# The vector engine in source order through the mixer of an encoder, with the convolution's taps between the pieces of weights

## The chip, the cores and the metric

The kernel runs on one core of a Trainium2 chip. A core has five engines that matter here, each with a queue of instructions of its own: TensorE (PE, matrix products and transposes), VectorE (DVE), ScalarE (ACT), GpSimd (POOL) and SyncE (SP, which issues most transfers). An engine works its queue strictly in order and waits on semaphores for what the others produce. The metric is the device time of one execution in microseconds, the median over several. Less is better.

## The reference

What is computed is a two-layer encoder over 256 tokens of width 1024, all in float32. One layer is a half step of a SwiGLU feed-forward block, the mixer, a second half step of feed-forward, and a gated embedding. The change lies in the mixer alone:

```python
u = rms_norm(h, norm_mix[i])
q, k, v, c, g = jnp.split(u @ w_in[i], splits, axis=-1)     # 512, 128, 128, 1024, 2048

q = rms_norm(q.reshape(B, S, N_HEADS, HEAD_DIM), q_norm[i])   # 8 heads of 64
k = rms_norm(k.reshape(B, S, KV_HEADS, HEAD_DIM), k_norm[i])  # 2 heads of 64
y_attn = window_attention(q, k, v, sink[i], rel_bias) @ w_attn_out[i]

c_val, c_gate = jnp.split(c, 2, axis=-1)
c = c_val * jax.nn.sigmoid(c_gate)
c = depthwise_conv(c, conv_w[i], conv_b[i])                   # 31 taps, 512 channels
c = jax.nn.silu(layer_norm(c, conv_ln_g[i], conv_ln_b[i]))
y_conv = c @ w_conv_out[i]

g_attn, g_conv = jnp.split(jax.nn.sigmoid(g), 2, axis=-1)
h = h + (g_attn * y_attn + g_conv * y_conv) @ w_o[i]
```

So attention and the convolution both come out of the same projection, run independently of each other, and meet in the last line.

## The kernel before

All products are float32 by three passes. Each weight is split into a high part, which ACT casts (`w_hi`, L104), and a low part, which DVE subtracts (`w_lo`, L105); PE then adds up high times high, low times high and high times low (L310 to L312). The class `Weights` streams the weights through this. A unit is one load of up to 1 MB into one of 5 raw buffers, issued by SP; a piece is half a unit or so, split into one of 8 pairs of `w_hi` and `w_lo`. Each `get()` prepares pieces up to 7 ahead of the one it hands out, and first runs the functions that were left with `later(n, fn)`, n calls earlier. The weights of attn_out and conv_out are used as they lie in their raw buffers, so such a buffer stays taken until PE has done with it.

The mixer, `mix`, runs in this order of source: two pieces of the convolution's input (`conv_in`, `ps_c`), queries (`ps_q`), keys and values (`ps_kv`), four chunks of gates (`ps_g`) into which the four blocks of attention are woven by `later` (scores `ps_s`, probabilities transposed `ps_pt`, products with the values `ps_o`), then attn_out (`ps_ao`), the layer norm of the convolution (transposes `ps_yt`, norm `yn`, transposes back `ps_yc`, a silu), conv_out (`ps_co`), and the merged product with w_o (`ps_up`), whose end prepares the second feed-forward block.

DVE has four kinds of work here. It subtracts the low parts. It runs the convolution: 30 taps for each of 4 groups of 128 channels (tap 0 goes to ACT), each a multiply-add over 256 tokens into `y`, 120 instructions a layer (L581). It normalizes the heads: a reduction, an addition, ten dependent small steps of an inverse square root (Newton's steps, `rh` and `nwt`), and four products, for q (`qn`) and for k (`kn`). And it runs the running maximum of the scores (L727) and the layer norm by token.

A scheduler orders the instructions of all engines at build time. It takes each instruction by a priority, which by default follows the source, and by a simulated time at which its operands are there. Before, two settings bend this in the mixer: the taps are given a priority 800 later than where they stand (`BACKGROUND`), and the preparation of weights one 100 later (`WEIGHTS_LAG`). The head norms and the layer norm run in `with_urgency`, which raises their priority.

Of the kernel before, what the change touches and what calls it, by code (L numbers as in the profile page):

```python
# [27 lines left out]
KC = CD // P  # L28
TAPS = 31
# [6 lines left out]
N = 512  # L36
LOOK = 7
RAW_BUFS = 5
BACKGROUND = 800
WEIGHTS_LAG = 100  # L40
ATTN = 5
W_BUFS = 8
DOWN_TAIL = 3
# [2 lines left out]
class Weights:  # L46
# [3 lines left out]
    def __init__(self, tc, raw_pool, w_pool):  # L50
        self.tc, self.nc = tc, tc.nc
        self.raw_pool, self.w_pool = raw_pool, w_pool
        self.units, self.specs = [], []
        self.raw, self.ready, self.held, self.hooks = {}, {}, {}, []
        self.next_load = self.next_prep = self.next_get = 0
        self.rest, self.pin, self.lag = 0, None, 0

    def unit(self, k, n, sources):
        self.units.append((k, n, sources))
# [24 lines left out]
    def prep_upto(self, i):  # L84
        nc = self.nc
        while self.next_prep <= min(i, len(self.specs) - 1):
            k, n, pieces, as_is = self.specs[self.next_prep]
            for u, *_ in pieces:
                self.load_upto(u + RAW_BUFS - 2)
                if u >= self.next_load:  # L90
                    return
            if as_is:
                ((u, k0, s0, _, w),) = pieces
                self.ready[self.next_prep] = (self.raw[u][:, k0 : k0 + k, s0 : s0 + w],)
                self.next_prep += 1
                continue
            hi = self.w_pool.tile([P, 2 * N], F32R, name="w_hi")
            lo = self.w_pool.tile([P, 2 * N], F32R, name="w_lo")
            hv = hi[:, : k * n].rearrange("p (k n) -> p k n", n=n)
            lv = lo[:, : k * n].rearrange("p (k n) -> p k n", n=n)  # L100
            for u, k0, s0, d0, w in pieces:
                src = self.raw[u][:, k0 : k0 + k, s0 : s0 + w]
                parts = (
                    nc.scalar.copy(out=hv[:, :, d0 : d0 + w], in_=src),  # L104
                    nc.vector.tensor_tensor(  # L105
                        out=lv[:, :, d0 : d0 + w],
                        in0=src,
                        in1=hv[:, :, d0 : d0 + w].bitcast(F32),
                        op=ALU.subtract,
                    ),  # L110
                )
                if self.pin:
                    for ins in parts:
                        self.pin(ins)
                    self.pin = None
            self.ready[self.next_prep] = (hv, lv)
            self.next_prep += 1

# [9 lines left out]
    def get(self):  # L128
        i = self.next_get
        due = [fn for at, fn in self.hooks if at <= i]  # L130
        self.hooks = [h for h in self.hooks if h[0] > i]
        for fn in due:
            fn()
        p0 = self.tc.cur_priority
        self.tc.cur_priority = p0 + self.lag
        self.prep_upto(i + LOOK - self.rest)
        self.tc.cur_priority = p0
        self.next_get += 1
        return self.ready.pop(i)


@with_exitstack
def encoder_kernel(ctx: ExitStack, tc: tile.TileContext, a: dict, out: bass.AP):
# [12 lines left out]
    def acc_tile(name):  # L156

        return accp.tile([P, NT, N], F32, name=name, tag="acc")
# [4 lines left out]
    def tok(t):  # L163
        return slice(t * P, (t + 1) * P)
# [45 lines left out]
    ws = Weights(tc, raw_pool, w_pool)  # L210
# [351 lines left out]
    def mix(l, st, nxt):  # L562
        u = st.x
        cw, kg, bias, sink = (late[n] for n in ("cw", "kg", "bias", "sink"))
        with tc.tile_pool(name="mix_pool", bufs=1) as mp:
            cpad = mp.tile([P, KC, T + 2 * PAD], F32, name="cpad", tag="cpad")
            nc.gpsimd.memset(cpad[:, :, 0:PAD], 0.0)
            nc.gpsimd.memset(cpad[:, :, PAD + T :], 0.0)
            y = mp.tile([P, KC, T], F32, name="y")
            background = tc.cur_priority + BACKGROUND  # L570
            ws.lag = WEIGHTS_LAG

            def tap(i, t):
                src = cpad[:, i, t : t + T]
# [11 lines left out]
            def conv_in(i):  # L586

                acc = acc_tile("ps_c")

                def evac():  # L590
                    cc = tmp.tile([P, NT, 256], F32, name="hh")
                    for t in range(NT):
                        sg = tmp.tile([P, 256], F32, name="sg")
                        nc.scalar.activation(out=sg, in_=acc[:, t, 256:], func=AF.Sigmoid, scale=st.rt(t))
                        nc.vector.scalar_tensor_tensor(
                            out=cc[:, t, :], in0=acc[:, t, :256], scalar=st.rt(t), in1=sg, op0=ALU.mult, op1=ALU.mult
                        )

                    def turn_c():
                        ps = tr_tile("ps_ct").rearrange("p (f t) -> p f t", f=2)  # L600
                        for f in range(2):
                            for t in range(NT):
                                nc.tensor.transpose(ps[:, f, tok(t)], cc[:, t, f * P : (f + 1) * P], ident)
                        nc.scalar.copy(out=cpad[:, i : i + 2, PAD : PAD + T], in_=ps)
                        p0 = tc.cur_priority
                        for t in range(TAPS):
                            for f in range(2):
                                tc.cur_priority = background + KC * t + i + f
                                tap(i + f, t)
                        tc.cur_priority = p0  # L610

                    ws.later(1, turn_c)

                chunk(acc, KD, u)
                pending.append(evac)
# [172 lines left out]
            def squash(c):  # L788
                for t in range(NT):
                    gs = g[:, t, c * N : (c + 2) * N]  # L790
                    tc.keep_in_program_order(nc.scalar.activation(out=gs, in_=gs, func=AF.Sigmoid))

            for c in range(4):
                gates(c)

# [12 lines left out]
            yn = mp.tile([P, NT, N], F32, name="yn", tag="pTs", bufs=2)  # L808

            def ln_by_token():  # L810
                for t in range(NT):
                    ps = tr_tile("ps_yt")
                    for i in range(KC):
                        nc.tensor.transpose(ps[:, i * P : (i + 1) * P], y[:, i, tok(t)], ident)
                    six = tmp.tile([P, 6], F32, name="six")
                    nc.vector.bn_stats(out=six, in_=ps)
                    mv = tmp.tile([P, 2], F32, name="mv")
                    nc.vector.bn_aggr(out=mv, in_=six)
                    rs = tmp.tile([P, 1], F32, name="rs")
                    nc.vector.tensor_scalar(  # L820
                        out=mv[:, 1:2], in0=mv[:, 1:2], scalar1=1e-5, scalar2=None, op0=ALU.add
                    )
                    rsqrt(rs, mv[:, 1:2], 1)
                    nc.vector.tensor_scalar(
                        out=yn[:, t, :], in0=ps, scalar1=mv[:, 0:1], scalar2=rs, op0=ALU.subtract, op1=ALU.mult
                    )
                table(AF.Silu)
# [59 lines left out]
                xs = x_tok[:, t, cols(c)]  # L887
                nc.vector.tensor_tensor(out=xs, in0=acc[:, t, :], in1=xs, op=ALU.add)

            ws.lag = 0  # L890
            return update(nxt(), KD, (Halves(ym[0]), Halves(ym[1])), add, 2)


# [119 lines left out]
```

## Time and profile before

| what | value |
|---|---|
| median of 3 runs | 1212.34 us (1212.13 to 1212.96) |
| the profiled execution's own time | 1212.65 us |
| its span | 1210.9 us |
| PE busy | 1155.3 us, 95% |
| DVE busy | 736.9 us, 61% |
| ACT busy | 583.2 us, 48% |
| TensorE's mean granted clock | 0.977 of full speed |
| mixer of layer 0, from the first `ps_c` to the second feed-forward's first product | about 214 to 391 us |

A row of a timeline gives the start in the span, the duration, engine, line, operation, the tile written and the tiles read, the shape, how many alike stand in a row, and in brackets how long the engine idled before and what ended that. Where an engine's rows stand close together, their durations overlap by a little, so a queue of them is shorter than the sum.

### The profile page before, as it was taken

How to read it: one execution, taken by the hardware profiler on the slowest of the kernel's cores; microseconds unless marked ns; L12 is line 12 of the kernel's file. 1: busy time of each engine (PE TensorE's matmuls, PEld its weight loads, DVE VectorE, ACT ScalarE, POOL GpSimd, SP SyncE). 2: the span in 40 equal slices, each digit the busy share in tenths (PEclk: the TensorE clock that was granted, in tenths of full speed). 3: DMA queues.
4: the chain of work that ended last, by engine and by line, in shares of the span. 5: the costliest groups of instructions: out<-in, count | busy, mean ns of one | idle time of the engine just before them, and what ended most of it. 6: DMA issues, size and time to landing. Idle time of an engine off the chain costs nothing.

```text
span 1210.9 us, 13444 instructions
## 1 busy us (share of the span) xinstructions
PE 1155.3 (95%) x5074; PEld 906.0 (75%) x5074; DVE 736.9 (61%) x1187; ACT 583.2 (48%) x803; POOL 5.7 (0%) x21
## 2 busy tenths in 40 slices
PE   8999999949999999999999999999399999999998
PEld 6878888836647888888878888888276588888786
DVE  7555554799546655555675555557994375555544
ACT  7444444525734544444555544446177255445432
POOL 0000000000000000000000000000000000000000
PEclk9999999978999999999999999999699999999999
DMA  9866555551354565555646555565323546555520
GB/s 318 275 207 213 180 170 186 182 137 35 105 164 157 180 189 188 158 190 173 209 150 198 182 183 191 176 195 162 94 70 104 173 151 200 180 183 178 178 87 35
DMA packets 155356, 202.47 MB, mean 167 GB/s; under 512 B 5283, under 2 KB 108787, under 8 KB 155292
## 3 DMA queue, kind: packets, MB, share of 16 engines
q1 hardware_dynamic: 154204, 200.57, 52.4%
q10 hardware_dynamic: 1088, 1.05, 0.3%
q8 instruction: 40, 0.66, 0.2%
q14 instruction: 24, 0.20, 0.1%
HBM read 200.53 MB, written 1.06 MB: 166 GB/s over the span
## 4 chain that ended last, share of the span: by engine, by line
PE 90%; DVE 7%; issue 1%; ACT 1%; DMA 1%; ACTq 0%; DVEq 0%
PE ps_gu L310 13%; PE ps_gu L312 13%; PE ps_gu L311 13%; PE ps_up L310 8%; PE ps_up L311 8%; PE ps_up L312 8%; DVE y L581 4%; PE ps_co L306 2%; PE ps_g L310 2%; PE ps_ao L306 2%; PE ps_g L311 2%; PE ps_g L312 2%; PE ps_h L521 2%; PE ps_s L718 2%; PE ps_x L358 1%; PE ps_pe L312 1%
## 5 line engine op out<-in xcount | busy, mean ns | idle before, releaser
L105 DVE TENSOR_TENSOR w_lo<-raw,w_hi 128x1024 fp32r<-128x1024 f32 x360 | 439.6, 1224 | 356.9 <-ACT w_hi L104 356.3
L104 ACT CAST w_hi<-raw 128x1024 fp32r<-128x1024 f32 x360 | 376.6, 1051 | 412.9 <-PE ps_gu L312 202.9
L311 PE MATMUL ps_up<-w_lo,hh 128*128 128x512 f32 x352 | 139.4, 396 | 0.0
L312 PE MATMUL ps_up<-w_hi,hl 128*128 128x512 f32 x352 | 139.4, 396 | 0.0
L310 PE MATMUL ps_up<-w_hi,hh 128*128 128x512 f32 x352 | 139.3, 396 | 0.0
L581 DVE SCALAR_TENSOR_TENSOR y<-cpad,cw,y 128x256 f32<-128x256 f32 x240 | 101.7, 478 | 0.0
L312 PEld LDWEIGHTS ps_up<-w_hi,hl 128*128 128x128 f32 x352 | 66.0, 188 | 16.1
L310 PEld LDWEIGHTS ps_up<-w_hi,hh 128*128 128x128 f32 x352 | 66.0, 188 | 15.8
L311 PEld LDWEIGHTS ps_up<-w_lo,hh 128*128 128x128 f32 x352 | 66.0, 188 | 15.7
L311 PE MATMUL ps_gu<-w_lo,x0h 128*128 128x512 f32 x176 | 70.6, 401 | 0.0
L312 PE MATMUL ps_gu<-w_hi,x0l 128*128 128x512 f32 x176 | 70.2, 399 | 0.0
L312 PE MATMUL ps_gu<-w_hi,xn0l 128*128 128x512 f32 x176 | 69.1, 395 | 1.2 <-DVE xn0l L348 1.2
L310 PE MATMUL ps_gu<-w_hi,x0h 128*128 128x512 f32 x176 | 69.9, 397 | 0.0
L311 PE MATMUL ps_gu<-w_lo,xn0h 128*128 128x512 f32 x176 | 69.6, 395 | 0.0
L311 PE MATMUL ps_gu<-w_lo,xf0h 128*128 128x512 f32 x176 | 69.5, 395 | 0.0
L311 PE MATMUL ps_gu<-w_lo,xf1h 128*128 128x512 f32 x176 | 69.5, 395 | 0.0
L310 PE MATMUL ps_gu<-w_hi,xn0h 128*128 128x512 f32 x176 | 69.2, 393 | 0.0
L310 PE MATMUL ps_gu<-w_hi,xf1h 128*128 128x512 f32 x176 | 69.1, 393 | 0.0
L310 PE MATMUL ps_gu<-w_hi,xf0h 128*128 128x512 f32 x176 | 69.1, 393 | 0.0
L312 PE MATMUL ps_gu<-w_hi,xf1l 128*128 128x512 f32 x176 | 69.0, 395 | 0.0
L312 PE MATMUL ps_gu<-w_hi,xf0l 128*128 128x512 f32 x176 | 69.0, 395 | 0.0
L513 DVE SCALAR_TENSOR_TENSOR hh<-ps_gu,r_x,sg 128x256 f32<-128x256 f32 x88 | 42.1, 479 | 3.5 <-ACT sg L512 3.5
(217 smaller groups left out, 1805.7 us busy)
## 6 DMA issues: line engine op xcount, KB each, us to landing
raw<-in_w_ffn_in_dram SPq DMA_DIRECT2D x172, 512.0 KB
raw<-in_w_ffn_out_dram SPq DMA_DIRECT2D x40, 1024.0 KB
raw<-in_w_in_dram SPq DMA_DIRECT2D x22, 1024.0 KB
raw<-in_w_in_dram SPq DMA_DIRECT2D x16, 512.0 KB
raw<-in_w_o_dram SPq DMA_DIRECT2D x8, 1024.0 KB
raw<-in_w_pe_gate_dram SPq DMA_DIRECT2D x8, 1024.0 KB
raw<-in_w_ffn_out_dram SPq DMA_DIRECT2D x8, 512.0 KB
raw<-in_w_attn_out_dram SPq DMA_DIRECT2D x8, 512.0 KB
```

The lines of the kernel that those rows point to most:

```text
L104: nc.scalar.copy(out=hv[:, :, d0 : d0 + w], in_=src),
L105: nc.vector.tensor_tensor(out=lv[:, :, d0 : d0 + w], in0=src, in1=hv[:, :, d0 : d0 + w].bitcast(F32), op=ALU.subtract,),
L306: nc.tensor.matmul(ps, x[:, kx, tok(t)], w[0][:, k, :], start=first, stop=last)
L310: nc.tensor.matmul(ps, xh, wh[:, k, :], start=first, stop=False)
L311: nc.tensor.matmul(ps, xh, wl[:, k, :], start=False, stop=False)
L312: nc.tensor.matmul(ps, xl, wh[:, k, :], start=False, stop=last)
L358: nc.tensor.transpose(v[:, f, i * P : (i + 1) * P], src[:, t, (k0 + f) * P : (k0 + f + 1) * P], ident)
L513: nc.vector.scalar_tensor_tensor(out=hh[:, t, :], in0=acc[:, t, 256:], scalar=x.rt(t), in1=sg, op0=ALU.mult, op1=ALU.mult)
L521: nc.tensor.transpose(ps[:, f, tok(t)], hh[:, t, f * P : (f + 1) * P], ident)
L581: nc.vector.scalar_tensor_tensor(out=y[:, i, :], in0=src, scalar=w, in1=y[:, i, :], op0=ALU.mult, op1=ALU.add)
L718: nc.tensor.matmul(ps[:, c, :], qT[v * HD : (v + 1) * HD, c, qb * P : (qb + 1) * P], kT[v * HD : (v + 1) * HD, :], start=True, stop=True,)
```

## The change

The mixer runs under a setting in which the scheduler leaves DVE's instructions in the order of the source; the other engines are ordered as before. The two settings that bent priorities go. The taps are no longer issued where the channels arrive: tap 0 (on ACT) is, and the other 30 of each group go to a list. After each `get()` a few of the list are issued: 3 up to the keys and values; from the gates on 5 where that call has split a piece of weights, and 8 where it hasn't. What is left is issued ahead of the layer norm by token. The number of instructions on each engine is the same.

```diff
-BACKGROUND = 800
-WEIGHTS_LAG = 100
...
     def get(self):
...
-        p0 = self.tc.cur_priority
-        self.tc.cur_priority = p0 + self.lag
+        n = self.splits
         self.prep_upto(i + LOOK - self.rest)
-        self.tc.cur_priority = p0
         self.next_get += 1
+        if self.each:
+            self.each(self.splits > n)
         return self.ready.pop(i)
...
     def mix(l, st, nxt):
-        with tc.tile_pool(name="mix_pool", bufs=1) as mp:
+        with tc.tile_pool(name="mix_pool", bufs=1) as mp, ExitStack() as order:
+            order.enter_context(tc.manual_schedule(engines={mybir.EngineType.DVE}))
...
-            background = tc.cur_priority + BACKGROUND
-            ws.lag = WEIGHTS_LAG
+            taps, rate = [], [3, 3]
+
+            def some_taps(split):
+
+                for _ in range(min(len(taps), rate[0 if split else 1])):
+                    taps.pop(0)()
+
+            ws.each = some_taps
...
                         nc.scalar.copy(out=cpad[:, i : i + 2, PAD : PAD + T], in_=ps)
-                        p0 = tc.cur_priority
-                        for t in range(TAPS):
-                            for f in range(2):
-                                tc.cur_priority = background + KC * t + i + f
-                                tap(i + f, t)
-                        tc.cur_priority = p0
+                        for f in range(2):
+                            tap(i + f, 0)
+                        taps.extend(lambda t=t, f=f: tap(i + f, t) for t in range(1, TAPS) for f in range(2))
...
+            rate[:] = 5, 8
             for c in range(4):
                 gates(c)
...
             def ln_by_token():
+                while taps:
+                    taps.pop(0)()
                 for t in range(NT):
...
-            ws.lag = 0
+            order.close()
+            ws.each = None
             return update(nxt(), KD, (Halves(ym[0]), Halves(ym[1])), add, 2)
```

How DVE's queue reads around the head norms of layer 0. Before, from the reduction for the queries on (`ms` is the mean square, `y` a tap):

```order
L636 TENSOR_REDUCE ms<-qn 128x16
L581 SCALAR_TENSOR_TENSOR y<-cpad,cw,y 128x256 x2
L105 TENSOR_TENSOR w_lo<-raw,w_hi 128x1024
L639 TENSOR_TENSOR ms<-ms,eps_x 128x16
L581 SCALAR_TENSOR_TENSOR y<-cpad,cw,y 128x256 x4
L105 TENSOR_TENSOR w_lo<-raw,w_hi 128x1024
L376 TENSOR_SCALAR rh<-ms 128x16
```

The same engine and place in the changed order, from the second conv piece's gate product (`hh`) to the reduction and its first small steps:

```order
L602 SCALAR_TENSOR_TENSOR hh<-ps_c,r_x,sg 128x256 x2
L104 TENSOR_TENSOR w_lo<-raw,w_hi 128x1024
L588 SCALAR_TENSOR_TENSOR y<-cpad,cw,y 128x256 x3
L104 TENSOR_TENSOR w_lo<-raw,w_hi 128x1024
L588 SCALAR_TENSOR_TENSOR y<-cpad,cw,y 128x256 x3
L104 TENSOR_TENSOR w_lo<-raw,w_hi 128x1024
L588 SCALAR_TENSOR_TENSOR y<-cpad,cw,y 128x256 x3
L104 TENSOR_TENSOR w_lo<-raw,w_hi 128x1024
L588 SCALAR_TENSOR_TENSOR y<-cpad,cw,y 128x256 x3
L640 TENSOR_REDUCE ms<-qn 128x16
L643 TENSOR_TENSOR ms<-ms,eps_x 128x16
L376 TENSOR_SCALAR rh<-ms 128x16
```

And, in the changed order, from the queries' last products to the reduction for the keys:

```order
L651 TENSOR_TENSOR qn<-ps_q,rh 128x4x64 x4
L104 TENSOR_TENSOR w_lo<-raw,w_hi 128x1024
L588 SCALAR_TENSOR_TENSOR y<-cpad,cw,y 128x256 x3
L104 TENSOR_TENSOR w_lo<-raw,w_hi 128x1024
L588 SCALAR_TENSOR_TENSOR y<-cpad,cw,y 128x256 x5
L640 TENSOR_REDUCE ms<-kn 128x4
```

Before, the two head norms ran side by side, one small step at a time, with two to four taps or a `w_lo` between steps. Now each head norm is one unbroken run, that of the keys behind that of the queries, and the taps and `w_lo` stand in blocks ahead of each.

DVE's queue at the end of the convolution. Before, from the last reciprocal of the softmax to the first layer norm, whose second follows after two more `w_lo`:

```order
L738 RECIPROCAL den<-den 128x4
L105 TENSOR_TENSOR w_lo<-raw,w_hi 128x1024 x2
L816 BN_STATS six<-ps_yt 128x6
L818 BN_AGGR mv<-six 128x2
```

Now:

```order
L742 RECIPROCAL den<-den 128x4
L588 SCALAR_TENSOR_TENSOR y<-cpad,cw,y 128x256 x40
L823 BN_STATS six<-ps_yt 128x6
L825 BN_AGGR mv<-six 128x2
```

And, now, the end of the second layer norm and what follows it:

```order
L831 TENSOR_SCALAR yn<-ps_yt,mv,rs 128x512
L104 TENSOR_TENSOR w_lo<-raw,w_hi 128x1024 x2
L808 TENSOR_TENSOR g<-ps_ao,g 128x512 x2
L104 TENSOR_TENSOR w_lo<-raw,w_hi 128x1024 x2
```

Before, the last taps stood ahead of the last block of scores. Now 40 taps of the second pair of channel groups stand between the last reciprocal and the layer norm, and the `w_lo` of w_o that stood ahead of and between the two layer norms stand behind both.

PE's queue at attn_out and the layer norm. Before (an entry of a product here is one matrix product, which the timeline of a profile shows as two passes):

```order
L306 MATMUL ps_ao<-raw,o 128x512
L758 MATMUL ps_o<-pTs,vt 64x512 x2
L306 MATMUL ps_ao<-raw,o 128x512
L814 MATMUL ps_yt<-ident,y 128x128 x4
L834 MATMUL ps_yc<-ident,yn 128x128
L306 MATMUL ps_ao<-raw,o 128x512 x13
L834 MATMUL ps_yc<-ident,yn 128x128 x7
L306 MATMUL ps_ao<-raw,o 128x512
L306 MATMUL ps_co<-raw,y 128x512 x12
L358 MATMUL ps_x<-ident,g 128x128 x4
```

Now:

```order
L306 MATMUL ps_ao<-raw,o 128x512 x2
L762 MATMUL ps_o<-pTs,vt 64x512 x2
L821 MATMUL ps_yt<-ident,y 128x128 x2
L306 MATMUL ps_ao<-raw,o 128x512 x12
L821 MATMUL ps_yt<-ident,y 128x128 x4
L306 MATMUL ps_ao<-raw,o 128x512 x2
L841 MATMUL ps_yc<-ident,yn 128x128 x8
L306 MATMUL ps_co<-raw,y 128x512 x12
L358 MATMUL ps_x<-ident,g 128x128 x8
```

The last four transposes of `ps_yt` (the second pair of channel groups, for both token tiles) have moved from ahead of most of attn_out to two products before its end, and the transposes of the normalized result from within attn_out to behind it.

On ACT, the last copy of the probabilities (`pTs`) stood ahead of two table loads, and the last copy of `o` between the two last sigmoids of the gates behind them; now one table load stands ahead of the copy of `pTs`, and the other one with both sigmoids between it and the copy of `o`. In FFN2's preparation, all 16 transposes of the new x now stand behind the last product of w_o, and one `w_lo` stands on DVE between the last addition to x and the scaling `xg` that the second feed-forward block waits for.

More of the change, by code (lines that the diff above doesn't have):

```diff
@@ L55, in __init__ @@
         self.next_load = self.next_prep = self.next_get = 0
-        self.rest, self.pin, self.lag = 0, None, 0
+        self.rest, self.pin = 0, None
+        self.splits, self.each = 0, None
     def unit(self, k, n, sources):
@@ L115, in prep_upto @@
                     self.pin = None
+            self.splits += 1
             self.ready[self.next_prep] = (hv, lv)
```

## The prediction

> **What bounds the kernel now.** I read the page first, then the waits of PE, windows around the longest wait, and at last the timelines of the mixer of layer 0.
>
> ```profile
> span 1210.9 us, 13444 instructions
> PE 1155.3 (95%) x5074; PEld 906.0 (75%) x5074; DVE 736.9 (61%) x1187; ACT 583.2 (48%) x803; POOL 5.7 (0%) x21
> ...
> PE 90%; DVE 7%; issue 1%; ACT 1%; DMA 1%; ACTq 0%; DVEq 0%
> ...
> L581 DVE SCALAR_TENSOR_TENSOR y<-cpad,cw,y 128x256 f32<-128x256 f32 x240 | 101.7, 478 | 0.0
> ```
>
> PE is busy for 95% of the span, so only PE's idle time, and time at a lower clock, can be won. DVE is 61% busy over all, yet stands for 7% of the chain; its taps (L581) are the suspects. The waits of PE say where:
>
> ```profile
> PE ps_qt L672 <- DVE qn L647: 16.4, 1, 16.4
> PE ps_qt L672 <- issue: 16.4, 1, 16.4
> PE ps_kt L697 <- DVE kn L647: 5.8, 2, 2.9
> ...
> PE ps_x L358 <- DVE g L870: 2.4, 2, 1.2
> ...
> PE ps_yc L834 <- ACT o L765: 1.3, 1, 1.3
> ```
>
> One wait of 16.4 us and one of 2.9 us stand in each layer, between the projections and the scores. The second 16.4 is put down to "issue", but it is the same transpose in the other layer. Windows (columns: window, length, then busy time of PE, PEld, DVE, ACT, POOL; then the granted clock, the share of DMA, GB/s) show who is busy there:
>
> ```profile
> 250.00:275.00 25.00, 5.70 (x23) 3.86 (x21) 25.00 (x77) 4.95 (x8) 0.00 (x0) 0.63 0.47 110
> 275.00:300.00 25.00, 24.45 (x91) 18.67 (x92) 24.43 (x70) 16.77 (x41) 0.56 (x1) 0.82 0.13 43
> 850.00:873.00 23.00, 3.67 (x16) 2.46 (x14) 23.00 (x73) 3.55 (x6) 0.00 (x0) 0.58 0.40 101
> ```
>
> DVE is full in all three; PE works 5.70 us of 25. The clock is low too, and finer windows show from where to where: full until 256, halved before 257, back at 284.
>
> ```profile
> 256.50:257.00 0.50, 0.00 (x0) 0.00 (x0) 0.50 (x2) 0.00 (x0) 0.00 (x0) 0.50 1.11 221
> 283.50:284.00 0.50, 0.50 (x3) 0.32 (x2) 0.50 (x3) 0.50 (x4) 0.00 (x0) 0.74 0.00 0
> ```
>
> PE's own rows around this stretch and at the mixer's end:
>
> ```profile
> 252.50 0.39 PE L312 MATMUL ps_g<-w_hi,xm0l 128*128 128x512 f32 x1
> 269.25 2.16 PE L672 MATMUL ps_qt<-ident,qn 128*128 128x128 f32 x8 [16.37 <-issue]
> 274.32 0.66 PE L697 MATMUL ps_kt<-ident,kn 128*128 128x128 f32 x2 [2.91 <-DVE kn L647]
> 275.55 3.78 PE L718 MATMUL ps_s<-kT,qT 64*128 64x256 f32 x8 [0.56 <-ACT kT L698]
> ...
> 331.21 1.02 PE L306 MATMUL ps_ao<-raw,o 128*128 128x512 f32 x2
> ...
> 348.19 0.93 PE L834 MATMUL ps_yc<-ident,yn 128*128 128x128 f32 x7
> ...
> 349.82 10.46 PE L306 MATMUL ps_co<-raw,y 128*128 128x512 f32 x24
> ```
>
> PE stops at 252.9; scores start at 275.55. The clock falls 3.6 us after the stop and is back 8.1 us after the restart. Those 8.1 us at half clock do 4 us of work: 4 us lost in layer 0 beside the waits, and I take as much for layer 1.
>
> **The change, part by part.** No instruction is added or removed; the order of DVE in the two mixers, and what the other engines make of it, is all. I walk DVE's queue of the changed order through layer 0, in the clock of this trace, with these rows:
>
> ```profile
> 230.90 2.36 DVE L105 TENSOR_TENSOR w_lo<-raw,w_hi 128x1024 fp32r<-128x1024 f32 x2 [0.45 <-ACT w_hi L104]
> ...
> 234.98 2.56 DVE L581 SCALAR_TENSOR_TENSOR y<-cpad,cw,y 128x256 f32<-128x256 f32 x6
> ...
> 237.46 1.22 DVE L636 TENSOR_REDUCE ms<-qn 128x16 f32<-128x1024 f32 x1
> ...
> 239.42 1.04 ACT L104 CAST w_hi<-raw 128x1024 fp32r<-128x1024 f32 x1
> ...
> 268.40 1.42 DVE L647 TENSOR_TENSOR qn<-ps_q,rh 128x256 f32<-128x256 f32 x4
> ...
> 273.82 0.62 DVE L647 TENSOR_TENSOR kn<-ps_kv,rh 128x64 f32<-128x64 f32 x4
> ...
> 326.76 0.15 DVE L377 TENSOR_SCALAR rs<-rs 128x1 int32<-128x1 int32 x1
> 326.95 0.16 DVE L379 TENSOR_TENSOR nwt<-rs 128x1 f32<-128x1 f32 x1
> ```
>
> Queued one behind the other, records overlap by some 0.08 us: a w_lo subtract takes 2.36 − 1.22 = 1.14, a tap (2.56 − 0.48)/5 = 0.4, and a small step that needs the one before it 0.19 (326.95 − 326.76).
>
> *A, queries.* DVE must first finish the gate product of the second conv piece, whose sigmoid now stands on ACT behind the square for the queries and two casts; the second of these is the row at 239.42, so the product ends about 240.4. Then come, in source order, 4 w_lo, 12 taps, the reduce, 12 small steps and 4 products: 4.5 + 4.7 + 1.1 + 2.3 + 1.4 = 14.1, so qn at 254.5. PE waits 1.6 instead of 16.4. Before, each small step had stood behind two taps (two taps are 0.8 us against 0.19).
>
> *B, keys.* Two w_lo, 8 taps, the reduce of k (shorter), 12 small steps and 4 products: 2.3 + 3.2 + 0.3 + 2.3 + 0.5 = 8.6, kn at 263.1. PE's 8 transposes of q take 1.1 at full clock, to 255.6: it waits 7.5 instead of 2.9. What is late next is thus k. Scores follow 1.1 later as before, at 264.2: **11.35 us ahead**.
>
> *C, clock.* PE idles 9 us of 10.6 here, long enough to fall to half again (3.6 sufficed). I keep the loss of 4 us; no gain.
>
> By the Trainium skill, "TensorE: Matmul & The Clock Gate", section "What's actually happening", an idle window of about 3.4 us halves the clock and one busy window of as much restores it. The fall after 3.6 agrees; the return after 8.1 does not, unless one counts from the dense ps_g after the scores. By the page's figure each fall would lose about 1.7 us, an estimate; with G at that instead of 2.8 the whole would come to 1216.8. The sum stays with the row.
>
> *D, to attn_out.* PE is full there, so the lead stays; two of four yt transposes move behind it (0.6): attn_out at 331.21 − 11.35 − 0.6 = 319.3.
>
> *E, attn_out.* Rows of ACT at the end of attention:
>
> ```profile
> 307.29 1.05 ACT L104 CAST w_hi<-raw 128x1024 fp32r<-128x1024 f32 x1 [1.20 <-DMA raw<-in_w_o_dram]
> ...
> 316.02 0.18 DVE L738 RECIPROCAL den<-den 128x4 f32<-128x4 f32 x1 [2.17 <-ACT s L734]
> ...
> 333.99 1.28 ACT L791 ACT_TABLE_LOAD   x1
> 335.28 1.06 ACT L791 ACTIVATE g<-g 128x1024 f32<-128x1024 f32 x1
> 336.25 0.57 ACT L765 COPY o<-ps_o 128x512 f32<-128x512 f32 x1
> ```
>
> The last copy of pTs now stands behind one table load (about 1.5 with its start), and the last copy of o behind another and both sigmoids: 1.3 + 2.0 + 0.6, less the 1.9 of PE's own o products, is about 1.9. So 3.4 us of waits, where the row of ps_yc had 1.3. PE's work from attn_out's start to conv_out's was 349.82 − 331.21 = 18.6; less that wait and 0.9 of yc, and with 0.3 more of yt, it is 16.7. Attn_out ends at T = 319.3 + 16.7 + 3.4 = 339.4: 10.4 ahead still.
>
> The last 40 taps stand ahead of the layer norm. They begin after the last reciprocal, which waits for ACT as before (316.02 − 307.29 = 8.7 us from the first w_o cast; I put it at 314.6), and take 16: y at 330.6. That is covered, since PE's order asks for the last four yt transposes only 12 products of attn_out later.
>
> *F, layer norm.* This is the price. The chain of one token tile and the loads of w_o:
>
> ```profile
> 321.10 2.36 DVE L105 TENSOR_TENSOR w_lo<-raw,w_hi 128x1024 fp32r<-128x1024 f32 x2 [4.90 <-ACT w_hi L104]
> ...
> 325.44 0.70 DVE L816 BATCH_NORM_STATS2 six<-ps_yt 128x6 f32<-128x512 f32 x1 [1.98 <-PE ps_yt L814]
> ...
> 328.46 2.00 ACT L104 CAST w_hi<-raw 128x1024 fp32r<-128x1024 f32 x2 [1.14 <-DMA raw<-in_w_o_dram]
> ...
> 329.55 2.36 DVE L105 TENSOR_TENSOR w_lo<-raw,w_hi 128x1024 fp32r<-128x1024 f32 x2
> ...
> 339.67 1.28 ACT L836 ACT_TABLE_LOAD   x1
> ```
>
> A chain takes 329.55 − 325.44 = 4.1. Before, one ran under attention and the other under attn_out. Now both token tiles' transposes end at T − 1.7 (two products of attn_out follow), so both chains run after them: yn at T + 6.5. A second path is longer: w_o's third load takes the buffer that attn_out's weights hold until T, because the w_lo that freed another one early now stand behind both norms. A load's time to its cast is 328.46 − 323.46 = 5.0; then 2.0 of casts, 1.3 of table and some 0.5 of the first silu (estimated from the 0.57 of o's copy): conv_out starts at T + 8.9 = 348.3 against 349.82, **1.5 ahead**.
>
> *G, clock again.* PE idles 6.5 us or more at a stretch, against the 3.6 that halved it. Conv_out pays: 4.4 us of dense work at half clock (279.3, where the rows of scores end and ps_g follows, to 283.7) would lose 2.2, the whole 8.1 lose 4.0. I take 2.8, nearer the first, because conv_out is dense: 1.3 behind.
>
> *H, into FFN2.*
>
> ```profile
> 387.14 1.28 DVE L367 TENSOR_TENSOR xg<-ps_x,par 128x512 f32<-128x512 f32 x2
> ```
>
> All of x's transposes now stand behind the last ps_up, and on DVE a w_lo stands between the last add and xg: add 0.6 (of xg's size), w_lo 1.1, xg 0.6 and a cast 0.5 (half of a w_hi) make 2.8; at least 1.7 if the w_lo falls under the transposes. I take 2.6, less the 1.2 of L870's wait, which 32 products now cover: 1.4.
>
> **Sum.** Layer 0: −11.35 − 0.6 + 2.4 (E's 3.4 and 0.3, less the 1.3 that was there) + 8.0 (F's 8.9, less yc's 0.9 that was there) + 2.8 + 1.4 = 2.7 slower. Layer 1 has the same stall (its window) but no wait of ps_yc before: 2.7 + 1.3 = 4.0. In all 6.7 against the profiled execution's 1212.65, which stood 0.3 above the median: **1219.0**. Bounds of the unknown: G 2.2 to 4.0, H 0.5 to 1.6, F 6.5 + 1 (no late load) to 8.9 + 2: per layer from −2.7 to +3.5 around it, so 1213.5 to 1226.
>
> **Rivals.** *1, the stall goes.* If DVE were ahead at both head norms, and the norms at the end stayed hidden, each layer would win 16.4 + 2.9 + 0.6 + 4 = 23.9: 1164.5. For it: the small steps no longer stand behind taps. Against: 14.1 and 8.6 us of queued work, and 120 taps a layer that must go somewhere. 0.05.
>
> *2, faster by part.* The second wait is interrupted by transposes, so the clock might stay (4.0 won per layer), and the load of w_o might come in time (1.4 won) with no second fall of the clock (2.8): 8.2 per layer, 1219.0 − 16.4 = 1202.6. For it: the lead of 11 us is certain to be large. Against: the idle stretch of 7.5 is twice what halved the clock. 0.20.
>
> *3, traded even.* No fall of the clock at the end only, 2.8 per layer: 1213.4. For it: yc's transposes come in between. 0.17.
>
> *4, slower still.* A w_o load comes 5.0 later and holds ACT, with the last exps behind its cast: the reciprocal, then the 40 taps, end at 335.6; it decides where they pass T − 2.3 = 337, else PE waits for the load's cast itself, up to 5.0 per layer: 1229. For it: the cast of 307.29 did wait for its DMA (1.20). Against: loads are asked for earlier in time, PE being ahead. 0.10.
>
> **The numbers.** The forecast has 0.48 and gives the time. What a measurement can tell from no change is 0.2%, 2.4 us. Faster: rivals 1 and 2 and a sixth of 3, 0.28. Same: the rest of 3 and the low end of the forecast, 0.17. Slower: 0.55. The range for 8 in 10 takes in 2 and 4 and leaves out 1: 1203 to 1229; the forecast's own is 1213.5 to 1226.
>
> **What would show it.** ps_qt waits about 2 us, ps_kt about 7.5, with scores 11 us earlier; the granted clock still dips to 0.5 there; ps_yc waits 5 us or more for yn (L831), and conv_out for y or a cast; a second dip of the clock in conv_out. The forecast is wrong if ps_kt's wait is under 4 us, if yn is ready before attn_out ends, or if w_o's third load lands before T.

## The result, and the profile after

The changed kernel takes **1220.12 us** (median of 4 runs, 1219.83 to 1223.14) against 1212.24 of the kernel before (4 runs, 1211.24 to 1212.96): a ratio of 1.0071, with a 95% interval of [1.0054, 1.0089]. It is slower, by 7.9 us; 1219.0 was forecast. The head of the page and its list of the chain of waits:

```profile
span 1218.1 us, 13445 instructions
...
PE 90%; DVE 6%; ACT 2%; DMA 1%; issue 1%; SPq 0%; DVEq 0%; ACTq 0%
```

PE's share of the chain is 90% in both kernels and does not tell them apart; the waits of PE do (total, times, longest):

```profile
PE ps_kt L701 <- DVE kn L651: 15.6, 2, 7.8
PE ps_yc L841 <- DVE yn L831: 11.8, 4, 3.6
PE ps_yt L821 <- ACT o L769: 3.7, 2, 1.9
...
PE ps_x L358 <- DVE xg L367: 3.3, 2, 1.6
PE ps_co L306 <- ACT y L843: 2.4, 2, 1.3
PE ps_o L762 <- ACT pTs L754: 2.4, 2, 1.2
PE ps_qt L676 <- DVE qn L651: 2.0, 3, 1.7
...
PE ps_qt L676 <- issue: 1.6, 1, 1.6
```

The 16.4 us per layer for the queries are 1.6; the keys cost 7.8 instead of 2.9. Five waits are new or longer, all between the end of attention and FFN2. PE's own rows of layer 0 show how the lead comes and goes:

```profile
253.71 0.41 PE L676 MATMUL ps_qt<-ident,qn 128*128 128x128 f32 x2 [1.62 <-issue]
...
263.01 0.66 PE L701 MATMUL ps_kt<-ident,kn 128*128 128x128 f32 x2 [7.81 <-DVE kn L651]
264.23 3.78 PE L722 MATMUL ps_s<-kT,qT 64*128 64x256 f32 x8 [0.56 <-ACT kT L702]
...
318.72 2.10 PE L306 MATMUL ps_ao<-raw,o 128*128 128x512 f32 x4
...
336.38 0.60 PE L821 MATMUL ps_yt<-ident,y 128*128 128x128 f32 x4
336.82 1.88 PE L306 MATMUL ps_ao<-raw,o 128*128 128x512 f32 x4
341.02 0.30 PE L841 MATMUL ps_yc<-ident,yn 128*128 128x128 f32 x1 [2.32 <-DVE yn L831]
344.91 1.75 PE L841 MATMUL ps_yc<-ident,yn 128*128 128x128 f32 x7 [3.60 <-DVE yn L831]
347.92 13.01 PE L306 MATMUL ps_co<-raw,y 128*128 128x512 f32 x24 [1.25 <-ACT y L843]
```

The scores start 11.3 us earlier than before (275.55), conv_out only 1.9 earlier (349.82), and its first 24 rows take 13.01 instead of 10.46. FFN2's first gated product comes at 392.38 instead of 390.52. DVE's rows point at the cause:

```profile
314.09 0.18 DVE L742 RECIPROCAL den<-den 128x4 f32<-128x4 f32 x1 [9.32 <-ACT s L738]
314.19 15.89 DVE L588 SCALAR_TENSOR_TENSOR y<-cpad,cw,y 128x256 f32<-128x256 f32 x40
336.80 0.70 DVE L823 BATCH_NORM_STATS2 six<-ps_yt 128x6 f32<-128x512 f32 x1 [6.72 <-PE ps_yt L821]
...
344.05 0.81 DVE L831 TENSOR_SCALAR yn<-ps_yt,mv,rs 128x512 f32<-128x512 f32 x1
```

DVE stands idle for 9.3 us ahead of the reciprocal with 40 taps queued behind it. They end at 330.1; then DVE idles again (6.7 us), until PE's queue comes to the four transposes, and both layer norms run with PE waiting.

### The profile page after: what moved, and what is told of

Its sections match the earlier page's. It is cut to its first block, busy times and chain, and to the rows that moved or that the text cites. A ratio compares the mean times of both kernels' runs of the same rounds, so it can differ in the third digit from the quotient of the medians.

```text
span 1218.1 us, 13445 instructions
## 1 busy us (share of the span) xinstructions
PE 1159.9 (95%) x5074; PEld 906.2 (74%) x5074; DVE 740.8 (61%) x1187; ACT 584.5 (48%) x803; POOL 3.7 (0%) x21
## 4 chain that ended last, share of the span: by engine, by line
PE 90%; DVE 6%; ACT 2%; DMA 1%; issue 1%; SPq 0%; DVEq 0%; ACTq 0%
PE ps_gu L312 13%; PE ps_gu L310 13%; PE ps_gu L311 13%; PE ps_up L310 8%; PE ps_up L311 8%; PE ps_up L312 8%; PE ps_co L306 3%; PE ps_g L310 2%; PE ps_g L311 2%; PE ps_g L312 2%; PE ps_ao L306 2%; DVE w_lo L104 2%; PE ps_h L521 2%; PE ps_s L722 2%; PE ps_pe L312 1%; PE ps_pe L310 1%
## 5 line engine op out<-in xcount | busy, mean ns | idle before, releaser
L588 DVE SCALAR_TENSOR_TENSOR y<-cpad,cw,y 128x256 f32<-128x256 f32 x240 | 98.3, 477 | 11.4 <-ACT y L584 11.3
L347 ACT CAST hh<-ps_h 128x512 fp32r<-128x512 f32 x44 | 25.8, 586 | 40.4 <-PE ps_h L521 40.4
```

Source lines behind the costliest of these rows:

```text
L347: nc.scalar.copy(out=hi, in_=src)
L588: nc.vector.scalar_tensor_tensor(out=y[:, i, :], in0=src, scalar=w, in1=y[:, i, :], op0=ALU.mult, op1=ALU.add)
```

## The experiments

All kernels compute the same result. The table has, in us, the time with its ratio to the kernel before, and from each profiled execution the start of scores and of conv_out in layer 0 and of FFN2's first gated product in both layers. A ratio is taken against runs of the kernel before from the same round (medians of 1211.93 to 1212.39), so it can differ a little from the quotient of two times in the table. Kernels 1 and 2 ran once; the others have 4 to 10 runs.

| kernel | time | ratio, 95% interval | scores | conv_out | FFN2, 0 | FFN2, 1 |
|---|---|---|---|---|---|---|
| before | 1212.24 | | 275.55 | 349.82 | 390.52 | 987.56 |
| changed | 1220.12 | 1.0071 [1.0054, 1.0089] | 264.23 | 347.92 | 392.38 | 994.16 |
| 1 no lag | 1211.23 (one run) | | 274.98 | 348.06 | 388.86 | 986.14 |
| 2 taps between | 1227.41 (one run) | | 276.90 | 351.14 | 396.75 | 1001.62 |
| 3 order ends ahead of conv_out | 1214.67 | 1.0024 [1.0013, 1.0035] | 264.37 | 347.84 | 389.53 | 989.58 |
| 4 order ends ahead of the norm | 1215.87 | 1.0034 [1.0021, 1.0046] | 264.70 | 348.21 | 391.19 | 989.84 |
| 5 23 taps early | 1212.34 | 1.0001 [0.9992, 1.0010] | 265.06 | 343.52 | 389.13 | 986.57 |
| 6 keys behind queries | 1221.52 | 1.0070 [1.0055, 1.0085] | 259.45 | 351.06 | 394.99 | 995.83 |
| 7 both | 1219.72 | 1.0058 [1.0042, 1.0075] | 259.50 | 347.25 | 392.86 | 994.84 |
| 8 squash late | 1216.02 | 1.0030 [1.0021, 1.0039] | 264.71 | 344.87 | 389.10 | 989.15 |
| 9 rates 7, 8 | 1216.29 | 1.0040 [1.0026, 1.0055] | 266.03 | 348.55 | 392.42 | 993.69 |
| 10 rates 8, 8, keys | 1215.05 | 1.0024 [1.0014, 1.0034] | 259.68 | 345.29 | 389.18 | 990.00 |
| 11 27 early, order ends | 1204.49 | 0.9940 [0.9925, 0.9955] | 264.73 | 344.13 | 385.35 | 979.13 |
| 12 23 early, 6, 8, order ends | 1198.84 | 0.9891 [0.9877, 0.9906] | 265.25 | 341.75 | 382.95 | 973.90 |

### 1 and 2: what made the stall

The kernel before, with `WEIGHTS_LAG = 0` instead of 100:

> The kernel before with the lag of the weights set to zero and the taps' background priority kept: one part of the change alone. Theory (the lead comes from DVE's order around the head norms, which reads the same here as before): the waits of 16.4 and 2.9 us stay, 1211 to 1214. Rival (the lag made the stall): the first wait shrinks by several us and the time with it, below 1205.

```profile
PE ps_qt L672 <- DVE qn L647: 16.4, 1, 16.4
...
PE ps_kt L697 <- DVE kn L647: 5.8, 2, 2.9
```

The waits for queries and keys stay at 16.4 and 2.9 us. The lag of the weights had no part in the stall. Then the changed kernel with two taps behind each Newton step of both head norms, much as the order of before read there:

```diff
+            between()   # behind each of a Newton round's three steps
...
-                rsqrt(r, ms, n)
+                rsqrt(r, ms, n, lambda: [taps.pop(0)() for _ in range(min(2, len(taps)))])
```

> The changed kernel with two taps behind each of the nine Newton steps of both head norms, 36 of the 40 that were left to the end. Theory (the wait of 16.4 us was made by taps between dependent steps): each norm takes 18 taps or 7.1 us more, qn comes 7.1 and kn 14.2 us later, ps_qt waits 8.7 and ps_kt 14.9 us, scores start at about 278; at the end the layer norm is hidden, which gives back some 9 us per layer: 1226 to 1234. Rival (DVE fills idle time with them, and the order inside the norms does not matter): ps_qt's wait stays near 1.6, and the time falls below 1212 since the end is free.

```profile
260.43 2.16 PE L679 MATMUL ps_qt<-ident,qn 128*128 128x128 f32 x8 [7.57 <-issue]
...
275.68 0.66 PE L704 MATMUL ps_kt<-ident,kn 128*128 128x128 f32 x2 [13.09 <-DVE kn L654]
```

The stall is back, 7.6 + 13.1 us, with scores as late as before. So the taps that DVE had to run before the norms' last steps made it (step A). That they stood between steps that need each other is not told apart here from their number: 18 taps in a block ahead of the norm would take DVE the same 7 us, and that was not run. The stretch from scores to conv_out is back too, at 74.2 us (before 74.3, changed kernel 83.7): with more taps done in the stall, the norms are hidden again. Yet the whole, in its one run, is 15 us slower than before: 4.9 us more pass from conv_out to FFN2 in layer 0, a fall of the clock in conv_out among them. These prices behind the norms come without any lead, so they belong to the order.

### 3 and 4: the prices behind attention, apart

The order of the source ends ahead of conv_out's products and not behind them:

```diff
+            order.close()
             for c in range(2):
                 acc = acc_tile("ps_co")
...
-            order.close()
             ws.each = None
```

> Step H by itself: the source's order for DVE ends ahead of conv_out and no longer behind it; all before that stands as in the changed kernel. The scheduler then brings two groups of the new x's transposes back in between the products, and DVE's scaling xg ahead of the w_lo. Theory (H costs 2 to 3 us a layer): conv_out starts within 0.5 of the changed kernel's 347.9, the stretch from there to FFN2's first gated product falls from 44.5 to 42 us in both layers, the waits for xg, ym_h and xf (1.6 + 0.9 + 0.8 in a layer) fall to about 1: 1215 us. Rival (those waits stand for products that come later anyway): the stretch stays at 44 to 44.5, 1219 to 1220 us.

From conv_out to FFN2 layer 0 now takes 389.53 − 347.84 = 41.7 us instead of 44.5. PE's row of conv_out:

```profile
347.84 11.43 PE L306 MATMUL ps_co<-raw,y 128*128 128x512 f32 x24
```

Conv_out loses 11.43 − 10.46 = 0.97 to the clock here and 2.55 in the changed kernel. Without these, the stretch is 40.7 here and 41.9 there (40.7 before): step H is worth **1.2 us**, and as much in layer 1 (42.39 − 1.66 here, 43.47 − 1.54 there); the other 1.6 us that this kernel wins in layer 0's stretch come from the clock, which was back at 349.6 and not at 352.9. The expected time was met, for less than half of it by the expected reason.

In the other kernel the order ends ahead of the layer norm, so that `w_lo` of w_o may stand ahead of the norms and a buffer for w_o's third load comes free early:

```diff
             def ln_by_token():
                 while taps:
                     taps.pop(0)()
+                order.close()
```

> Step F's two paths apart: the source's order for DVE ends ahead of the layer norm by token, so the w_lo of w_o need not stand behind both norms, and w_o's third load need not wait for attn_out's buffer. Both norms stay behind attn_out, as the taps still end behind its transposes' place. H goes with it. Theory (the longer path was the load's, and the norms' own stands right behind it): the cast of the third load no longer waits for its DMA, conv_out starts about 1 us earlier only, at T + 8 instead of T + 9.2, and with H at 2.5 a layer the whole is 1213 us. Rival A (the load's path was all of it): conv_out 2.5 us earlier, 1210 us. Rival B (the norms' path was all of it, and H is worth nothing): 1219 us.

ACT's rows, where the late load had cost 4.7 us of waiting for DMA ahead of the silu, and PE's:

```profile
327.42 1.99 ACT L103 CAST w_hi<-raw 128x1024 fp32r<-128x1024 f32 x2 [0.88 <-DMA raw<-in_w_o_dram]
...
336.79 1.99 ACT L103 CAST w_hi<-raw 128x1024 fp32r<-128x1024 f32 x2 [7.38 <-DMA raw<-in_w_o_dram]
...
347.60 1.93 ACT L844 ACTIVATE y<-ps_yc,par 128x256 f32<-128x256 f32 x4 [7.52 <-PE ps_yc L842]
```

```profile
338.88 0.60 PE L822 MATMUL ps_yt<-ident,y 128*128 128x128 f32 x4
346.03 0.45 PE L842 MATMUL ps_yc<-ident,yn 128*128 128x128 f32 x1 [6.54 <-DVE yn L832]
```

The third load is cast at 327.42 instead of 344.00, and the row at 336.79 is already the fourth's. The silu waits 7.52 for PE instead: conv_out starts no earlier (348.21), now by the norms' path alone. But this is not the norms' path of the changed kernel. The scheduler also put the four transposes behind all of attn_out, at 338.88 instead of 336.38, and on DVE four products with the gates and two `w_lo` stand between the taps and the norms, which begin at 341.34 instead of 336.80. So the kernel shows that the edit wins nothing at conv_out, and not that the two paths were equally long. The changed kernel's own row bounds it: there PE waited 1.25 us for the silu after the last transposes back, so without the late load at most about that could have been won, near the 1 us that the theory gave. On H the rival that called it worthless was wrong, since the layer's stretch to FFN2 is 1.5 us shorter with a fall of the clock in both.

### 5: the taps from behind the reciprocal to ahead of it

```diff
+                if (qb, v) == (1, 1):
+                    for _ in range(min(len(taps), 23)):
+                        taps.pop(0)()
                 nc.vector.reciprocal(out=den, in_=den)
```

> 23 of the 40 taps that stand between the last reciprocal and the layer norm move ahead of that reciprocal, where DVE idles 9.3 us. Theory (the price at the end is the two layer-norm chains that run after attn_out): y is ready 9 us earlier, all yt transposes stand ahead of most of attn_out, both chains run under it, conv_out starts some 2 us after attn_out ends instead of 9, and the clock does not fall there: 8 us per layer less than the changed kernel, about 1204. Rival (the late load of w_o sets conv_out's start): conv_out still starts 8 to 9 us after attn_out, about 1219.

DVE and PE, in the new order:

```profile
305.91 9.19 DVE L588 SCALAR_TENSOR_TENSOR y<-cpad,cw,y 128x256 f32<-128x256 f32 x23
315.33 0.18 DVE L745 RECIPROCAL den<-den 128x4 f32<-128x4 f32 x1 [0.23 <-ACT s L738]
```

```profile
325.14 1.93 PE L765 MATMUL ps_o<-pTs,vt 128*64 128x512 f32 x4 [3.32 <-ACT pTs L757]
...
327.75 0.66 PE L824 MATMUL ps_yt<-ident,y 128*128 128x128 f32 x4 [0.31 <-ACT o L772]
...
343.52 12.26 PE L306 MATMUL ps_co<-raw,y 128*128 128x512 f32 x24 [2.22 <-ACT y L846]
```

The idle time of 9.3 us takes the 23 taps almost for nothing (the reciprocal comes 50.3 us behind the scores instead of 49.9), both norms run under attn_out and ps_yc waits for nothing. The place of the 40 taps is thus shown as the cause of step F, for both of its paths at once: the norms are hidden, and the casts of w_o's third load, at 344.71, now stand behind the silu; and the slowdown is gone (ratio 1.0001). But 1204 was expected and 1212.34 measured: conv_out came 4.4 us earlier and 3 us behind attn_out, because ACT's queue is next:

```profile
320.55 1.28 ACT L389 ACT_TABLE_LOAD   x1
321.84 1.28 ACT L798 ACT_TABLE_LOAD   x1
...
324.09 0.99 ACT L757 COPY pTs<-ps_pt 128x1024 f32<-128x1024 f32 x1
...
339.59 1.99 ACT L103 CAST w_hi<-raw 128x1024 fp32r<-128x1024 f32 x2 [11.90 <-DMA raw<-in_w_o_dram]
341.60 1.28 ACT L846 ACT_TABLE_LOAD   x1
342.90 1.93 ACT L846 ACTIVATE y<-ps_yc,par 128x256 f32<-128x256 f32 x4
```

The last pTs stands behind two table loads and a sigmoid; the silu behind the casts of w_o's second load, which wait for it, and a table. Those 2.22 us of idle PE were enough to halve the clock at 344.3 (conv_out's 24 rows take 12.26, 1.8 lost).

### 6 and 7: a longer lead

No taps between queries and keys, so that the keys come sooner:

```diff
+                rate[:] = 0, 0
                 chunk(acc, KD, u, n=256)
...
             keys_values()
+            flush()
```

> No taps are issued in the keys' calls, and the norm of k is issued ahead of the gates' first call: between qn and the reduction of k there stands one w_lo instead of two w_lo and 8 taps. Theory (DVE's queue alone sets the second wait): kn comes 4.3 us earlier, ps_kt's wait falls from 7.8 to 3.5 us, and if that is too short for the clock to fall, 3.4 us more are won: scores 4.3 us ahead of the changed kernel. At the end 48 taps instead of 40 wait, but the transposes of yt move behind all of attn_out, which costs up to 1.7 us. Together 2.6 to 7.7 us per layer: 1205 to 1215, middle 1210. Rival (something else holds PE there): 1220.

```profile
258.08 0.81 PE L701 MATMUL ps_kt<-ident,kn 128*128 128x128 f32 x2 [3.52 <-DVE kn L651]
...
321.86 3.67 PE L764 MATMUL ps_o<-pTs,vt 128*64 128x512 f32 x4 [4.26 <-ACT pTs L756]
...
326.69 14.33 PE L306 MATMUL ps_ao<-raw,o 128*128 128x512 f32 x28
```

The wait is 3.5 as expected, so DVE's queue alone sets it, and the scores come 4.8 us earlier; the clock fell in that wait all the same, at 255.9, 1.3 us into it. Yet conv_out comes 3.1 us later, and 1221.52 was measured against 1210 expected. The last pTs again stood behind two tables and the sigmoids (4.26), the clock fell at 320.8 (attn_out's 28 rows take 14.33, where 28 undisturbed ones take 12.18 in kernel 10), and the norms, still behind attn_out, cost 4.15 + 3.44. Then with the 23 early taps as well:

> Both edits: the norm of k right behind that of q, and 23 taps ahead of the last reciprocal. Theory (two prices, independent): about 8 plus 5 us per layer less than the changed kernel, 1194. Rival (in this order ACT's last normalization of the probabilities stands behind two table loads and two sigmoids, 4.6 us, which PE then waits for at the end of attention): 1200 to 1204.

```profile
322.97 0.48 PE L757 MATMUL ps_pt<-ident,s 128*128 128x128 f32 x1 [6.36 <-ACT s L749]
```

Here PE waits 6.36 for the probabilities, whose normalization stands on ACT behind two tables and two sigmoids, as the rival said; but at 1219.72 its price was too small as well. In that wait the clock falls (at 320.2), and in conv_out it falls again after 2.24 us for the silu.

### 8 to 10: ACT's order, and DVE's room

Kernel 5 with the sigmoids of the last two gate pieces (`squash(2)`) behind the convolution's silu; then with rates of 7 and 8 from the gates on; then with 8 and 8 and the keys of kernel 6:

```diff
                         )
+                squash(2)
...
             squash(0)
-            squash(2)
```

> The early flush, and beside it the last two sigmoids of the gates move behind the silu of the convolution on ACT, so that no table load and sigmoid stands ahead of the last copies of pTs and o, and none ahead of the silu. Theory (with the layer norm hidden, what is left at the end is ACT's queue): PE's wait for pTs falls from 3.3 to about 1, the wait for y from 2.2 to about 1 (the load of w_o still ends there, with four casts ahead of the silu), and the clock does not fall: 4 to 5 us per layer less than the early flush, 1203. Rival (PE waits for the load of w_o whatever ACT does, and the four casts hold the silu): conv_out starts 5 us or more after attn_out, 1211 or more.

PTs waits 1.08, as expected, but the scheduler now put the four transposes of y behind ten products of attn_out, ps_yc waited 0.60 + 3.58 for the norm, and the clock fell: 1216.02, a miss.

> As the run before, and 7 instead of 5 taps behind each split piece in the gates, so that no tap is left after the last reciprocal and y is ready before attn_out starts. Here all yt transposes stand ahead of attn_out, and only two casts of w_o ahead of the silu. Theory (DVE idles 5.7 us of 25 under the gates and takes the taps there for nothing): both layer norms end within attn_out, conv_out starts 1 to 2 us after it, 5 to 6 us per layer less than the early flush, 1201. Rival (the taps delay the running maxima and the low parts, and PE waits in the gates): 1208 to 1215.

> As the run before with 8 taps behind each piece, and the norm of k right behind that of q. Theory (the scores start 4.7 us earlier, and now nothing at the end takes that back): 1190 to 1194. Rival (DVE is full from the scores to the layer norm, so that the running maxima come late): 1200 to 1206.

The longest of PE's waits in kernel 10:

```profile
PE ps_pt L757 <- ACT s L749: 15.5, 5, 4.7
```

With 7 or 8 taps per piece, DVE reaches the maxima of the softmax late, behind up to 24 taps in layer 0, and PE waits for the probabilities inside attention: 15.5 us over both layers here, 5.6 for ps_pt with rates of 7. Not all of it is DVE's: the last of these waits in layer 0 of kernel 10 (2.96 us, to 325.4) ends 6 us after the reciprocal, as the normalization stands on ACT behind the gates' scaling and a table load. Conv_out then runs without a fall of the clock and with the norms hidden, but starts at 345 to 349; in kernel 9 the clock had fallen ahead of attn_out, at 324.8. Both kernels missed their theories (1201, and 1190 to 1194) and came out above their rivals' ranges too (1208 to 1215, and 1200 to 1206). In these two, the lead ahead of attention was worth no more than the room that DVE had left in it.

### 11 and 12: the prices together

Kernel 8, with the order ended ahead of conv_out as in kernel 3; kernel 11 takes 27 early taps, kernel 12 keeps 23 and takes rates of 6 and 8:

```diff
-            rate[:] = 5, 8
+            rate[:] = 6, 8
...
+                if (qb, v) == (1, 1):
+                    for _ in range(min(len(taps), 23)):
+                        taps.pop(0)()
...
+                squash(2)
...
-            squash(2)
...
+            order.close()
             for c in range(2):
                 acc = acc_tile("ps_co")
```

> The same with rates of 5 and 8 and 27 taps ahead of the reciprocal in one block, so that the taps fall where the probabilities are waited for and not into the gates. Theory (only the place of the taps behind the gates decides): the reciprocal 1.6 us later than with 23, hidden under attn_out; the transposes of y ahead of attn_out's last 12 products, conv_out at 342 to 343, stretch 42: 1202 us. Rival (whatever starts earlier is given back before conv_out, by the clock or by ACT's queue): conv_out at 344 to 345, and only H's 2 to 3 us a layer is won on the 1212 of the kernel with 23 early taps and the 1216 of the one with the later squash: 1207 to 1212 us.

> What the runs so far point to, in one: 23 taps ahead of the reciprocal (norms hidden), the squash of the last two gate chunks behind the convolution's silu, 6 and 8 taps per piece from the gates on (the transposes of y ahead of attn_out's last 12 products), and the source's order ended ahead of conv_out (H). Theory: pTs waits about 1 instead of 3.3, no table load ahead of the silu, conv_out at 342 and without a fall of the clock, the stretch from there to FFN2's gated products 42: gains on the kernel with 23 early taps of 2 + 2 + 2 us a layer, 1201 us. Rival (DVE is full through the gates, so the extra taps there delay the maxima and the probabilities and PE waits in attention for what it gains behind it): conv_out at 345 to 347, 1211 to 1214 us.

Kernel 11's wait for the last probabilities, and kernel 12, PE from the last probabilities on:

```profile
321.93 0.33 PE L755 MATMUL ps_pt<-ident,s 128*128 128x128 f32 x1 [3.18 <-ACT s L747]
```

```profile
324.82 1.93 PE L765 MATMUL ps_o<-pTs,vt 128*64 128x512 f32 x4 [0.86 <-ACT pTs L757]
...
327.42 0.66 PE L824 MATMUL ps_yt<-ident,y 128*128 128x128 f32 x4 [0.68 <-ACT o L772]
327.92 10.47 PE L306 MATMUL ps_ao<-raw,o 128*128 128x512 f32 x24
...
341.75 10.57 PE L306 MATMUL ps_co<-raw,y 128*128 128x512 f32 x24 [0.78 <-ACT y L846]
...
353.92 0.63 PE L358 MATMUL ps_x<-ident,g 128*128 128x128 f32 x4 [1.60 <-DVE g L880]
```

In kernel 12 no wait there is over 1.6 us, and the clock, after its fall at the keys, stays full to FFN2; the stretch from conv_out is 41.2 us. The theory said 342 and 42, and 1201 for the whole: 1198.84 was measured, **1.1% faster than the kernel before** and, by the medians, 1.7% than the changed one. Kernel 11, between its theory and its rival at 1204.49, is 5.7 us slower than kernel 12: ACT took the gates' scaling and a table load ahead of the last normalization, PE waited 3.18 for it, and the clock fell at 323.1. Which of the rate and the place of the order's end did more for kernel 12 was not run apart.

## Why the prediction was right

The forecast, 1219.0 with slower at 0.55, held, and so did its shape: a lead of 11 us given back in five places. By its steps, layer 0 unless said:

- **A, queries**: qn at 254.5 expected, 254.3 measured; PE waits 1.6 as expected. Kernel 2 shows the reason, the taps queued within the norms.
- **B, keys**: kn at 263.1 expected and measured; wait 7.5 and 7.8; scores at 264.2 in both. That what is late next is the keys held exactly.
- **C, clock**: it fell in the wait, as said. Counted as the prediction did, from the start of scores (264.23) to the return (270.95), 3.4 us were lost in layer 0 against the 4 that were kept. In layer 1 it was 4.6 (scores at 865.98, return at 875.1). Rival 2, which needed the clock to stay, fell here.
- **D, attn_out**: 319.3 expected, 318.72 measured.
- **E**: pTs 1.5 expected and 1.20 measured, o 1.9 and 1.86; attn_out's end at 339.4 and 338.70. The last reciprocal came at 314.1 (314.6) and the taps ended at 330.1 (330.6). Rival 4, in which they pass attn_out, did not come.
- **F, the layer norm**: the transposes did end 1.7 us ahead of attn_out's end, and yn came 6.2 behind it (6.5 expected). The late load was the longer path, as priced: ACT's two casts began 5.3 behind (5.0), and conv_out started at 347.92 (348.3). What the prediction did not say is that the shorter path need not stay shorter when the longer one is cut: kernel 4 took the late load away, the norms moved later, and conv_out started no earlier.

```profile
344.00 1.99 ACT L103 CAST w_hi<-raw 128x1024 fp32r<-128x1024 f32 x2 [4.73 <-DMA raw<-in_w_o_dram]
```

- **G, clock again**: 2.8 expected, 2.55 lost in layer 0 and 12.00 − 10.46 = 1.54 in layer 1. One figure for both was a weak point of the sum: the loss goes with a phase (below), and 0.97 to 2.55 were seen in conv_out in this kernel and kernel 3.
- **H, into FFN2**: 1.4 expected, 1.2 by kernel 3. In other orders the stretch was longer: kernels 9 and 10 take 43.9 us there without a fall of the clock, kernel 12, with the order ended ahead, 41.2.

The sum for layer 0 was 2.7, measured 1.86 (392.38 − 390.52); for layer 1 4.0, measured 4.74; together 6.7 and 6.6. The span grew by 7.2 and the median by 7.9. Layer 1 was taken as a copy of layer 0, and that did not hold: counted from the first product of layer 0's FFN2, its scores came 9.8 us ahead and not 11.35, and conv_out 2.1 us behind instead of 0.2 ahead; a smaller G and H (1.54 and 1.1) took part of that back. So errors cancelled within layer 1 and between the layers, and that the forecast came within 1.1 us of the result is partly luck. The bounds of the sum are off by a few tenths too: its own terms give −2.9 to +3.4 a layer. Rival 1 (the stall goes altogether) failed on the keys, rival 3 on G.

## What to carry to other kernels

When a fixed order removes a stall, the work that filled the stall must find room elsewhere; look in the trace for where that engine now idles with such work queued behind a wait (here 9.3 us ahead of one reciprocal), and move the work ahead of that wait, in the amount that fits. A lead at one place is worth only what the next queues (here ACT's tables and sigmoids, then a load that needs a buffer) let through, so repair them together and count the idle stretches: one of 2.2 us cost the clock in kernel 5. End a manual order where its reason ends.

## What the runs showed of the hardware

TensorE's clock falls and returns on a grid. In the changed kernel, the half-microsecond windows in which it changes (columns as before; PEclk, third from the end, is the mean in the window):

```profile
257.00:257.50 0.50, 0.00 (x0) 0.00 (x0) 0.50 (x1) 0.00 (x0) 0.00 (x0) 0.79 0.00 0
270.50:271.00 0.50, 0.50 (x2) 0.40 (x2) 0.50 (x2) 0.00 (x0) 0.00 (x0) 0.55 1.05 197
342.50:343.00 0.50, 0.00 (x0) 0.00 (x0) 0.43 (x3) 0.00 (x0) 0.00 (x0) 0.63 1.04 406
352.50:353.00 0.50, 0.50 (x2) 0.18 (x1) 0.50 (x2) 0.50 (x1) 0.00 (x0) 0.63 1.10 326
```

The windows beside them read 1.00 on one side and 0.50 on the other, so a mean between gives the moment in the window: 257.29, 270.95, 342.63 and 352.87. The distances, 13.66, 71.68 and 10.24, are 4, 21 and 3 times 3.414. The kernel before fits as well (256.45 to 283.76 is 8 times 3.414). This is the free-running window of the Trainium skill, "TensorE: Matmul & The Clock Gate", "What's actually happening", which also says that the phase differs from run to run. The traces agree: the grids of the two kernels lie 0.84 us apart. The prediction had read the page's two figures without the phase; its estimate from them, 1.7 us a fall, stands against 2.55 and 1.54 in conv_out. What the runs add to the prediction's 3.6 us: an idle stretch of 2.22 us was enough in kernel 5, at 344.3, so a window need not be idle throughout. The place on the grid counts as well: in kernel 2, PE's wait of 2.20 us ahead of layer 0's conv_out halved the clock at 351.7, and the longer one of 2.40 us in layer 1, from 955.3 to 957.7, did not; by 177 steps from 351.7, a line of the grid at 955.9 cuts that stretch in two. And the clock did not come back in the first window after a restart where that held scores, whose tiles fill 64 of 128 rows; in the changed kernel and the one before it came back at the end of the first window that the dense products filled, or nearly. No run tested that by itself, so it is a reading of these traces and not shown.
